# Two plain query outputs ahead of ten factored pairs, and one page group in eight issued by ScalarE

## The chip, the cores and the metric

The kernel runs on one core of a Trainium2 chip. The core has a matrix engine (TensorE, PE in the profile) with its own weight loads (PEld), a vector engine (VectorE, DVE), an activation engine (ScalarE, ACT), a general engine (GpSimd, POOL) and a sync engine (SyncE, SP) that here only issues DMAs. DMAs are issued from SP, ACT or POOL. Each engine takes its instructions strictly in the order in which the program lists them for it. TensorE writes to PSUM, of which there are eight banks; everything else lives in SBUF or in DRAM.

The metric is the device time of one execution in microseconds. Before the change it is 1930.89, the median of three runs from 1927.16 to 1934.16.

## The reference, cut to what matters

One layer of a decoder, for 1024 prompt rows and 32 sample rows (8 sequences of 4), so R = 1056 rows of width 1024:

```python
h = rmsnorm(x, g_norm1) * (1 + scale1) + shift1
za, zq, zkv, zg, zm = jnp.split(h @ w_in, SPLIT_IDX, axis=-1)
u, v = jnp.split(jax.nn.gelu(za), 2, axis=-1)            # gated by W_s: ya
q = zq.reshape(B, T, B_HEADS, HEAD_DIM)
yb = nsa_attention(q, kv_rows, win_rows, ...)            # compressed, selected, window
gate_a, gate_b = jnp.split(jax.nn.sigmoid(zm), 2, axis=-1)
mixed = (gate_a * (ya @ w_branch_a) + gate_b * (yb @ w_branch_b)) @ w_out
x = x + gate1 * mixed
h2 = rmsnorm(x, g_norm2) * (1 + scale2) + shift2         # then ConvFFN, final norm
```

For the sample rows the attention looks at a paged cache: 64 pages of 128 rows for each of 8 sequences. Every 64 rows of two of its four slots go through a small network (`compress_blocks`: a sum over the 64 rows with w1, a gelu, then w2), which gives one compressed key and value per block. The kernel must read all 512 pages for that, 128 KB each.

## The kernel before, in words

All large products are done in float32 precision out of two rounded parts: x = hi + lo, w = hi + lo, and three matmuls hi·hi, hi·lo, lo·hi. `split` and `weight_parts` make the parts: a cast on ScalarE (L332), a subtraction on VectorE (L333). h is kept as eight tiles of hi and eight of lo (`hh`, `hl`), 128 rows of the contraction each and 1056 columns.

An output tile is 128 output features by 1056 columns. `dense` computes one plainly: three column chunks of 384, 384 and 288 (`CH`), eight tiles of h, three matmuls each. The four u tiles are made so (L701 to L724), and each is then multiplied by the spatial gate on GpSimd (L721) and stored (L722).

After them come 22 output tiles in pairs: 4 of queries, 16 of merge gates, 2 of keys. `pair` (L874) computes two output tiles together by a factored form. It cuts the contraction into two halves and the first 608 columns into two blocks of `HQ` = 304, so that h has four blocks B11, B12, B21, B22, and it forms seven block products in place of eight: with B11, B21, B22, with a sum block that takes B12's place, and with three more sum blocks T2, T3, T4. The last 448 columns are done plainly (`rest`). Each block product is 12 matmuls of 304 columns, so a pair has 84 of these and 48 of 448 columns. The sums over weights (s1 to s4) are made on GpSimd.

The sums over h do not exist when the pairs begin. `sums_of(k)` (L825) makes T2, T3 and T4 for one of four tiles; `last_sums` (L841) then overwrites B12 in place, after which a plain product over these columns is no longer possible. Each sum is cut into parts again by `parts_into` (L822 on ScalarE, L823 on VectorE). The first pair therefore has an order of its own (`opening`): all plain products first, with the sums built meanwhile, then the products that need sums. The last pair, the keys, also has its own order (`closing`).

Page loading is the other strand. There are 16 compression steps (L554), each over 32 pages, with one page buffer `st` for all of them. `step(n)` (L662) does compression n on TensorE (128 matmuls), its gelu on ScalarE (L569), and then calls `compress_load(n + 1)`. `load_pages` (L516) reads page numbers four at a time into registers (L528) and issues four DMAs (L538); `share` says which groups of four, by their running number modulo eight, ScalarE issues in place of SP: groups 1, 4 and 6 for steps 0 to 3, none for later ones. Groups on ScalarE are ordered behind the gelu of the step before. Each gelu result `g` is used at the start of the next compression (`compress_end`).

SBUF is divided into pools. `S` has 24 slots of 1056 columns; while the pairs run, 16 hold h, 4 hold w1 and 2 the compressed keys and values, so two are free. `W` holds weights: raw tiles, hi and lo. Before the pairs the old `W` is released and a new one with 4 raw, 3 hi and 3 lo tiles takes its place. `TR` holds T2 to T4, two tiles for weight sums, and one further tile `o` of 1056 columns: `out_tile` gives the two outputs of a pair out of the free slots and this tile in turn, so three places in all. An output's place comes free when its store from POOL's queue has landed.

TensorE's order in this part is set by a planner: it goes through the program with a cost model and puts at each point the first instruction of the text that the model holds to be ready. In the attention part the order is written out by hand (`manual_schedule`), where `later(steps, wait)` delays a piece by a count of columns; `US` is 2265 columns.

After the pairs come key tiles (eight copies on ScalarE, L1014 and L1015), the last compression (15), loads of queries and values on SP (L1038, L1051, L1054), and the first attention tile with its scores and exponentials (L1310).

Of the kernel before, what the change touches and what calls it, by code (L numbers as in the profile page):

```python
# [15 lines left out]
R = 1056  # L16
# [3 lines left out]
HQ = 304  # L20
# [33 lines left out]
def step_kernel(tc, A):  # L54
# [51 lines left out]
    def slot(dt=F32):  # L106
        return S([128, R], dt, "S", NS)
# [408 lines left out]
    def load_pages(items, after=None, share=(1, 4, 6), depth=2):  # L516
# [3 lines left out]
        for n in range(0, len(items), 4):  # L520
# [19 lines left out]
            starts.append(d)  # L540

    hidden = []

    paged = {}

    def compress_load(n):
        b, half = n // 2, n % 2
        home = "a"
        st = PG([128, 32, 256], F32, "st", 1)
        load_pages([(st[:, i], A["pcmp"], b * 64 + half * 32 + i) for i in range(32)], freed.get(home),  # L550
                   (1, 4, 6) if n < 4 else ())
        paged[n] = st, home
# [14 lines left out]
    def compress_act(n, ps, home):  # L567
        g = small(128, "pa", 3).rearrange("p (h c) -> p h c", h=2) if n == 15 else PG([128, 2, 64], F32, "g", 1)
        freed[home] = act.activation(g.rearrange("p h n -> p n h"), ps[:, 0:128].rearrange("p (n h) -> p n h", h=2),  # L569
                                     AF.Gelu_apprx_tanh, bias=b1t)  # L570
        hidden.append((n, g))
# [154 lines left out]
    RV.release()  # L726
    W.release()
    W = new_pool("weights2", "right")
    TR = new_pool("tr", "right")
# [9 lines left out]
    YCW = C2([128, 2, 128])  # L739

    def small(w, tag, bufs):
        return C2([128, w], F32, tag, bufs)

# [67 lines left out]
    f32 = lambda x: (x[0].bitcast(F32), x[1].bitcast(F32))  # L811
    homes = [0]

    def out_tile():
        homes[0] += 1
        return TR([128, R], F32, "o", 1) if homes[0] % 3 == 0 else slot()

    def sum_tile(i):
        return TR([128, 512], F32, f"sum{i}", 1)

# [3 lines left out]

    def sums_of(k, e):  # L825

        (h11, l11), (h12, l12), (h21, l21), (h22, l22) = (f32(x[k]) for x in (B11, B12, B21, B22))
        t = TR([128, R], F32, "o", 1)
        f0, f1, d = (t[:, HQ * i:HQ * i + HQ] for i in range(3))
        pool.tensor_tensor(d, l22, l12, op=OP.subtract)  # L830
        dve.tensor_tensor(f0, h22, h12, op=OP.subtract)
        dve.tensor_tensor(f0, f0, d, op=OP.add)
        dve.tensor_tensor(f1, f0, h11, op=OP.add)
        dve.tensor_tensor(f1, f1, l11, op=OP.add)
        parts_into(f1, *T2[k])
        pool.tensor_tensor(e, h21, f1, op=OP.subtract)
        pool.tensor_tensor(e, e, l21, op=OP.add)
        parts_into(f0, *T3[k])
        parts_into(e, *T4[k])

    def last_sums():  # L841

        t = TR([128, R], F32, "o", 1)
        for k in range(4):
            (h11, l11), (h12, l12) = (f32(x[k]) for x in (B11, B12))
            g, d = (t[:, c:c + HQ] for c in ((0, HQ), (HQ, 2 * HQ))[k % 2][0:1] + (2 * HQ,))
            pool.tensor_tensor(d, l12, l11, op=OP.subtract)
            dve.tensor_tensor(g, h12, h11, op=OP.subtract)
            dve.tensor_tensor(g, g, d, op=OP.add)
            parts_into(g, *B12[k])  # L850

    def weight_parts(x):
        hi, lo = (W([128, 512], F32R, tag, 3) for tag in ("hi", "lo"))
        split(x, hi, lo)
        return [[t[:, c:c + 128] for c in range(0, 512, 128)] for t in (hi, lo)]
# [10 lines left out]

    def pair_load(m, n):
        raws = []
        for j, c in ((m, 0), (n, 0), (n, 512), (m, 512)):
            raws.append(W([128, 512], F32, "raw", 4))  # L870
            pool.dma_start(raws[-1], A["w_t"][j][:, c:c + 512])  # L871
        return raws

    def pair(raws, ev, opening=False, closing=False):  # L874

        a11, a21, a22, a12 = raws
        g, t = out_tile(), out_tile()
        first, second, third = slice(0, HQ), slice(HQ, 2 * HQ), slice(2 * HQ, R)
# [16 lines left out]
        yield t, g  # L895
        if opening or closing:
            quarter_products(weight_parts(a21), rest[0:4], plain[1], True, False)
        if opening:
            quarter_products(weight_parts(a22), rest[4:8], plain[1], False, True)
            ev(g[:, third], plain[1])  # L900
            yield
        if not (opening or closing):
# [7 lines left out]
        if closing:  # L910
# [19 lines left out]
            return  # L930
        if opening:
            quarter_products(weight_parts(s2), T2, S, True, True)
            add(t[:, second], S, g[:, first])
        quarter_products(weight_parts(s3), T3, S, False, True)
# [6 lines left out]
        ev(g[:, 0:2 * HQ], g[:, 0:2 * HQ])  # L941
        if not opening:
            quarter_products(w, rest[4:8], plain[1], False, True)
            ev(g[:, third], plain[1])
        quarter_products(weight_parts(s4), B22, Z, False, True)
# [33 lines left out]

    n = 5  # L980
    PAIR = [(4, 5), (6, 7)] + [(10 + 2 * i, 11 + 2 * i) for i in range(8)] + [(9, 8)]
    raws = pair_load(*PAIR[0])
    for i in range(11):
        fn, ev, base = ((query, scaled, 4) if i < 2 else (merge_gate, gate, 10) if i < 10 else
                        (key, lambda o, x: act.copy(o, x), 8))
        work = pair(raws, ev, i == 0, i == 10)
        tiles = next(work)
        if i == 0:
            for k in range(4):
                sums_of(k, tiles[k % 2][:, HQ:2 * HQ])  # L990
            next(work)
            last_sums()
        if i < 10:
            step(n)
            n += 1
        next(work)
        if i < 10:
# [4 lines left out]
        if i in (5, 6, 7, 8):  # L1002
            next(first_blocks, None)
# [17 lines left out]
    def queries(i, l, qf=None):  # L1021
# [15 lines left out]
    qf = slot()[:, 0:512]  # L1037
    sync.dma_start(qf.rearrange("p (j c) -> p j c", j=4),  # L1038
                   q_d[:, :, 128 * TILES[0]:128 * TILES[0] + 128].rearrange("j p c -> p j c"))
    q_first = queries(TILES[0], None, qf)  # L1040
# [8 lines left out]
    qt = [slot() for _ in range(4)]  # L1049
    for j in range(4):  # L1050
        sync.dma_start(qt[j], q_d[j])  # L1051
    VV = [slot(), slot()]
    for i in range(2):
        sync.dma_start(VV[i][:, 0:1024].rearrange("p (k c) -> p k c", c=256),  # L1054
                       A["o_rows"][1][512 * i:512 * i + 512].rearrange("(k p) c -> p k c", p=128))

# [460 lines left out]
    with tc.manual_schedule(engines={mybir.EngineType.PE}):  # L1517
# [6 lines left out]

        later(ending(), US)
        for n in range(len(units) + AHEAD):
# [571 lines left out]
```

## Time and profile before

| | us |
|---|---|
| median of three runs | 1930.89 |
| lowest, highest | 1927.16, 1934.16 |
| profiled execution | 1926.18 |
| its span on the core | 1924.6 |
| TensorE busy in the span | 1828.4 |
| VectorE, ScalarE, GpSimd busy | 1243.1, 840.1, 636.5 |
| granted TensorE clock, mean | 0.988 |

The span runs from the first to the last instruction of the profiled execution; times inside it are counted from its start. A group row gives the source line, engine, operation and operand shapes, the count, then the busy time and the mean duration of one in ns, then the idle time of the engine just before these instructions with what ended it. Matmuls overlap in the pipeline, so the mean of one is longer than the distance between two. A timeline row gives start, length, the first instruction of a run of them, the count, and in brackets the idle time before. In the chain, SPq is the queue of the sync engine: it issues DMAs and is not counted as busy. A stage row gives busy times, the granted clock, the mean busy share of the 16 DMA engines, and GB/s.

### The profile page before, as it was taken

What the parts mean: (1) busy time and instruction counts of PE and PEld (TensorE: products, weight loads), DVE (VectorE), ACT (ScalarE), POOL (GpSimd) and SP (SyncE); (2) the same over time, 40 slices, a digit from 0 to 9 for tenths busy, and PEclk for the clock granted to TensorE, in tenths of its full rate; (3) what the DMA queues carried; (4) which work ended last, traced back from release to release, by engine and by line L of the source; (5) the groups of instructions that cost most, each with busy time, mean ns of one, the idle gap of its engine ahead of it and who ended that gap; (6) DMA issues with size and microseconds to landing.
All of it is one profiled execution on the core that took longest, in us unless ns stands there. A gap on an engine that the chain in (4) does not pass through costs nothing.

```text
span 1924.6 us, 43777 instructions
## 1 busy us (share of the span) xinstructions
PE 1828.4 (95%) x15905; PEld 1701.1 (88%) x15905; DVE 1243.1 (65%) x2547; ACT 840.1 (44%) x1707; POOL 636.5 (33%) x849
## 2 busy tenths in 40 slices
PE   5999989999998999999999999899999999999997
PEld 3999978998997776767789999899999999999997
DVE  7525265233335776776665778999988888757464
ACT  4313122233224654656652366544444444555343
POOL 2410253222232123222211411578766665301010
PEclk8999999999998999999999999999999999999998
DMA  9545455565659678867754455133322222767463
GB/s 335 191 141 173 155 174 185 178 221 187 219 195 300 223 230 288 276 224 237 251 185 179 146 165 170 56 123 123 95 88 76 87 76 93 264 209 231 127 197 104
DMA packets 239031, 345.35 MB, mean 179 GB/s; under 512 B 35264, under 2 KB 173408, under 8 KB 236640
## 3 DMA queue, kind: packets, MB, share of 16 engines
q1 hardware_dynamic: 205936, 260.48, 42.7%
q0 software_dynamic: 21328, 69.70, 10.6%
q10 hardware_dynamic: 11552, 12.37, 2.1%
q8 instruction: 126, 2.06, 0.4%
q14 instruction: 89, 0.73, 0.1%
HBM read 305.17 MB, written 41.43 MB: 180 GB/s over the span
## 4 chain that ended last, share of the span: by engine, by line
PE 73%; DVE 8%; DMA 6%; SPq 4%; issue 4%; ACT 3%; POOL 1%; DVEq 0%; ACTq 0%; POOLq 0%
PE t L63 70%; SPq L538 4%; PE t L67 3%; DVE t L333 2%; DMA t<-pcmp 1%; DMA t<-w_ada 1%; DMA t<-t 1%; DMA t<-psel 1%; ACT t L332 1%; DVE t L1730 1%; DVE t L1853 1%; SPq L528 1%; ACT t L1310 0%; DMA t<-w_t 0%; ACT t L1339 0%
## 5 line engine op out<-in xcount | busy, mean ns | idle before, releaser
L63 PE MATMUL t<-t,t 128*128 128x264 f32 (+12 forms) x15130 | 1754.2, 305 | 78.5 <-DVE t L184 16.2
L63 PEld LDWEIGHTS t<-t,t 128*128 128x128 f32 (+2 forms) x14970 | 1619.8, 168 | 153.8 <-issue 59.5
L333 DVE TENSOR_TENSOR t<-t,t 128x512 fp32r<-128x512 f32 (+5 forms) x523 | 433.6, 836 | 203.9 <-ACT t L332 197.3
L332 ACT CAST t<-t 128x512 fp32r<-128x512 f32 (+5 forms) x589 | 339.1, 593 | 497.5 <-PE t L63 351.4
L67 PEld LDWEIGHTS t<-t,t 128*128 128x128 f32 x746 | 81.0, 143 | 32.3 <-issue 9.0
L1778 DVE TENSOR_TENSOR t<-t,t 128x264 f32<-128x264 f32 (+2 forms) x296 | 92.1, 345 | 26.7 <-PE t L63 23.9
L67 PE MATMUL t<-t,t 128*128 128x128 f32 x746 | 106.5, 278 | 3.0 <-ACT t L1377 1.5
L538 POOL DMA_DIRECT2D t<-psel x128 | 70.6, 552 | 71.7 <-DMA t<-psel 29.2
L881 DVE TENSOR_TENSOR t<-t,t 128x304 f32<-128x304 f32 x55 | 25.9, 473 | 102.1 <-PE t L63 98.7
L1932 POOL TENSOR_TENSOR t<-t,t 128x384 f32<-128x384 f32 (+1 forms) x12 | 14.0, 1198 | 223.2 <-ACT t L1999 223.2
L1339 ACT COPY t<-t 128x512 f32<-128x512 f32 (+1 forms) x112 | 59.6, 569 | 35.3 <-PE t L67 35.2
L1309 DVE TENSOR_REDUCE t<-t 128x1 f32<-128x640 f32 (+3 forms) x64 | 58.8, 920 | 24.4 <-PE t L63 24.0
L1731 DVE SCALAR_TENSOR_TENSOR t<-t,t,t 128x1072 f32<-128x1072 f32 x44 | 74.5, 1692 | 0.0
L1730 DVE SCALAR_TENSOR_TENSOR t<-t,t,t 128x1072 f32<-128x1072 f32 x44 | 69.6, 1582 | 1.9 <-ACT t L1729 1.8
L1729 ACT ACTIVATE t<-t,t 128x1072 f32<-128x1072 f32 x44 | 56.8, 1290 | 31.5 <-DVE t L1778 22.9
L1310 ACT ACTIVATE t<-t,t 128x640 f32<-128x640 f32 (+3 forms) x64 | 56.3, 880 | 23.2 <-DVE t L1309 20.8
L1835 POOL TENSOR_TENSOR t<-t,t 128x1024 f32<-128x1024 f32 x22 | 54.6, 2481 | 20.5 <-ACT t L1834 20.5
L1366 POOL COPY t<-t 128x256 f32<-128x256 f32 x32 | 12.9, 404 | 133.8 <-DVE t L1364 61.4
L871 POOL DMA_DIRECT2D t<-w_t x44 | 24.6, 559 | 93.9 <-DVE t L333 76.9
L569 ACT ACTIVATE t<-t,t 128x128 f32<-128x128 f32 x16 | 7.9, 493 | 99.4 <-PE t L63 99.4
L721 POOL TENSOR_TENSOR t<-t,t 128x512 f32<-128x512 f32 (+1 forms) x12 | 12.1, 1025 | 115.6 <-ACT t L332 86.9
L1609 POOL TENSOR_TENSOR t<-t,t 128x384 f32<-128x384 f32 (+1 forms) x24 | 27.9, 1167 | 64.6 <-DVE t L1608 61.4
(294 smaller groups left out, 1421.0 us busy)
## 6 DMA issues: line engine op xcount, KB each, us to landing
t<-pcmp SPq DMA_DIRECT2D x464, 128.0 KB
t<-psel SPq DMA_DIRECT2D x384, 128.0 KB
t<-w_down SPq DMA_DIRECT2D x120, 256.0 KB
t<-t POOLq DMA_DIRECT2D x54, 528.0 KB, 3.8
t<-w_up SPq DMA_DIRECT2D x96, 256.0 KB
t<-psel POOLq DMA_DIRECT2D x128, 128.0 KB, 3.9
t<-w_ada SPq DMA_DIRECT2D x16, 1024.0 KB
t<-w_out SPq DMA_DIRECT2D x48, 256.0 KB
```

What stands on the lines that cost most here:

```text
L63: return pe.matmul(out, lhsT, rhs, start=start, stop=stop, skip_group_check=skip)
L67: return pe.transpose(out, x, ident)
L332: act.copy(hi, t)
L333: dve.tensor_tensor(lo, t, hi.bitcast(F32), op=OP.subtract)
L538: d = queue.dma_start(dst, src[bass.ds(r, 1)].rearrange("g p c -> p (g c)"))
L1309: dve.tensor_reduce(m4[:, branch, h:h + 1], ps[:, :, 0:w], axis=AX.XY, op=OP.max, negate=True)
L1310: act.activation(P[:, 0:L].rearrange("p (a c) -> p a c", a=2), ps[:, :, 0:w], AF.Exp, bias=m4[:, branch, h:h + 1], accum_out=s4[:, branch, ...
L1339: (act.copy if w > 2 else dve.tensor_copy)(probs[branch, h][:, 128 * k:128 * (k + w)], pt[:, c:c + 128 * w])
L1729: act.activation(acc[:, 0:w], up[:, 0:w], AF.Identity, scale=cw[:, n, 0:1], bias=cw[:, n, 3:4])
L1730: dve.scalar_tensor_tensor(acc[:, 0:w], up[:, 1:1 + w], cw[:, n, 1:2], acc[:, 0:w], op0=OP.mult, op1=OP.add)
L1731: dve.scalar_tensor_tensor(acc[:, 0:w], up[:, 2:2 + w], cw[:, n, 2:3], acc[:, 0:w], op0=OP.mult, op1=OP.add)
L1778: dve.tensor_tensor(o, by4(banks[c][:, c0:c0 + n], n), other(c, c0, n), op=OP.add)
```

## The change

The sums over h are no longer built inside a pair. Query outputs 4 and 5 are computed plainly (`plain_output`), half of the contraction at a time, and `sums_of` is called after each half; `last_sums` follows the second output. Compression 5 stands between the two. Ten pairs follow, the first of them queries 6 and 7; `pair` loses its opening order. In pair 0 compression 6 stands after the second group of products, and in pairs 1 to 8 compressions 7 to 14 stand after the first group.

The weight pool is not released: the pairs use the pool of the dense outputs, with 4 raw, 4 hi and 4 lo tiles of 524 columns. The tile `o` is gone: outputs of a pair and the scratch of the sums all come from the free slots. The differences that T4 is cut from go into the two weight-sum tiles.

From load 4 on, group 1 of each eight is issued by ScalarE. Every gelu result takes the tag `pa` of the small tiles, as only the last one did. The loads of queries and values are ordered behind the gelu of compression 14, and the small step that ends compression 15 is due 6 x US columns into attention and not 1 x US.

```diff
         load_pages([(st[:, i], A["pcmp"], b * 64 + half * 32 + i) for i in range(32)], freed.get(home),
-                   (1, 4, 6) if n < 4 else ())
+                   (1, 4, 6) if n < 4 else (1,))
...
-        g = small(128, "pa", 3).rearrange("p (h c) -> p h c", h=2) if n == 15 else PG([128, 2, 64], F32, "g", 1)
+        g = small(128, "pa", 3).rearrange("p (h c) -> p h c", h=2) 
...
-    W.release()
-    W = new_pool("weights2", "right")
     TR = new_pool("tr", "right")
...
-    def out_tile():
-        homes[0] += 1
-        return TR([128, R], F32, "o", 1) if homes[0] % 3 == 0 else slot()
...
-        t = TR([128, R], F32, "o", 1)
+        t = slot()
         f0, f1, d = (t[:, HQ * i:HQ * i + HQ] for i in range(3))
+        e = sum_tile(k % 2)[:, 0:HQ]
...
-        hi, lo = (W([128, 512], F32R, tag, 3) for tag in ("hi", "lo"))
+        hi, lo = (W([128, WP], F32R, tag, 4)[:, 0:512] for tag in ("hi", "lo"))
...
+    def plain_output(raws, ev, between):
+        out = slot()
+        banks = [pA()[:, 0:b - a] for a, b in CH]
+        for half in range(2):
+            w = weight_parts(raws[half])
+            for (a, b), ps in zip(CH, banks):
+                x = [(hh[k][:, a:b], hl[k][:, a:b]) for k in range(4 * half, 4 * half + 4)]
+                quarter_products(w, x, ps, half == 0, half == 1)
+                if half:
+                    ev(out[:, a:b], ps)
+            between(half)
+        return out
...
-        g, t = out_tile(), out_tile()
+        g, t = slot(), slot()
...
-    PAIR = [(4, 5), (6, 7)] + [(10 + 2 * i, 11 + 2 * i) for i in range(8)] + [(9, 8)]
+    plain_raws = raw_weights(((4, 0), (4, 512), (5, 0), (5, 512)))
+    query(0, plain_output(plain_raws[0:2], scaled, lambda half: sums_of(half)))
+    step(5)
+    query(1, plain_output(plain_raws[2:4], scaled, lambda half: sums_of(2 + half)))
+    last_sums()
+    PAIR = [(6, 7)] + [(10 + 2 * i, 11 + 2 * i) for i in range(8)] + [(9, 8)]
     raws = pair_load(*PAIR[0])
-    for i in range(11):
+    for i in range(10):
...
+        work = pair(raws, ev, i == 9)
+        next(work)
+        if 0 < i < 9:
+            step(6 + i)
+        next(work)
         if i == 0:
+            step(6)
...
+    fourteen = freed["a"]
+    with behind([fourteen]):
+        sync.dma_start(qf.rearrange("p (j c) -> p j c", j=4),
...
-        later(ending(), US)
+        later(ending(), US * 6)
```

More of the change, by code (lines that the diff above doesn't have):

```diff
@@ L540, in load_pages, with small @@
             starts.append(d)
+    def small(w, tag, bufs):
+        return C2([128, w], F32, tag, bufs)
     hidden = []
@@ L739, in step_kernel @@
     YCW = C2([128, 2, 128])
-    def small(w, tag, bufs):
-        return C2([128, w], F32, tag, bufs)
     def blocks(gr, bank):
@@ L811, in step_kernel @@
     f32 = lambda x: (x[0].bitcast(F32), x[1].bitcast(F32))
-    homes = [0]
-    def out_tile():
-        homes[0] += 1
-        return TR([128, R], F32, "o", 1) if homes[0] % 3 == 0 else slot()
-    def sum_tile(i):
-        return TR([128, 512], F32, f"sum{i}", 1)
+    sum_tile = lambda i: TR([128, 512], F32, f"sum{i}", 1)
     def parts_into(x, hi, lo):
@@ L823, in parts_into, with sums_of @@
         dve.tensor_tensor(lo, x, hi.bitcast(F32), op=OP.subtract)
-    def sums_of(k, e):
+    def sums_of(k):
         (h11, l11), (h12, l12), (h21, l21), (h22, l22) = (f32(x[k]) for x in (B11, B12, B21, B22))
-        t = TR([128, R], F32, "o", 1)
+        t = slot()
         f0, f1, d = (t[:, HQ * i:HQ * i + HQ] for i in range(3))
+        e = sum_tile(k % 2)[:, 0:HQ]
         pool.tensor_tensor(d, l22, l12, op=OP.subtract)
@@ L841, in last_sums @@
     def last_sums():
-        t = TR([128, R], F32, "o", 1)
+        t = slot()
         for k in range(4):
@@ L865, in step_kernel, with raw_weights, pair_load, pair @@
     rest = [tuple(t[:, 2 * HQ:R] for t in (hh[k], hl[k])) for k in range(8)]
-    def pair_load(m, n):
+    def raw_weights(items):
         raws = []
-        for j, c in ((m, 0), (n, 0), (n, 512), (m, 512)):
-            raws.append(W([128, 512], F32, "raw", 4))
+        for j, c in items:
+            raws.append(W([128, WP], F32, "raw", RAWS)[:, 0:512])
             pool.dma_start(raws[-1], A["w_t"][j][:, c:c + 512])
         return raws
-    def pair(raws, ev, opening=False, closing=False):
+    def pair_load(m, n):
+        return raw_weights(((m, 0), (n, 0), (n, 512), (m, 512)))
+    def plain_output(raws, ev, between):
[10 more added lines that the diff above has]
+        return out
+    def pair(raws, ev, closing=False):
         a11, a21, a22, a12 = raws
-        g, t = out_tile(), out_tile()
+        g, t = slot(), slot()
         first, second, third = slice(0, HQ), slice(HQ, 2 * HQ), slice(2 * HQ, R)
@@ L895, in pair @@
         yield t, g
-        if opening or closing:
+        if closing:
             quarter_products(weight_parts(a21), rest[0:4], plain[1], True, False)
[L898 to L902, printed above, removed]
+        else:
             quarter_products(weight_parts(s2), T2, S, True, True)
@@ L930, in pair @@
             return
-        if opening:
-            quarter_products(weight_parts(s2), T2, S, True, True)
-            add(t[:, second], S, g[:, first])
         quarter_products(weight_parts(s3), T3, S, False, True)
@@ L941, in pair @@
         ev(g[:, 0:2 * HQ], g[:, 0:2 * HQ])
-        if not opening:
-            quarter_products(w, rest[4:8], plain[1], False, True)
-            ev(g[:, third], plain[1])
+        quarter_products(w, rest[4:8], plain[1], False, True)
+        ev(g[:, third], plain[1])
         quarter_products(weight_parts(s4), B22, Z, False, True)
@@ L978, in key @@
                 pool.dma_start(A["o_wsk"][b][:, 508:512], kr[:, NP + 4 * b:NP + 4 * b + 4])
-    n = 5
-    PAIR = [(4, 5), (6, 7)] + [(10 + 2 * i, 11 + 2 * i) for i in range(8)] + [(9, 8)]
+    plain_raws = raw_weights(((4, 0), (4, 512), (5, 0), (5, 512)))
[4 more added lines that the diff above has]
+    PAIR = [(6, 7)] + [(10 + 2 * i, 11 + 2 * i) for i in range(8)] + [(9, 8)]
     raws = pair_load(*PAIR[0])
-    for i in range(11):
-        fn, ev, base = ((query, scaled, 4) if i < 2 else (merge_gate, gate, 10) if i < 10 else
+    for i in range(10):
+        fn, ev, base = ((query, scaled, 4) if i < 1 else (merge_gate, gate, 10) if i < 9 else
                         (key, lambda o, x: act.copy(o, x), 8))
-        work = pair(raws, ev, i == 0, i == 10)
-        tiles = next(work)
-        if i == 0:
[L989 to L997, printed above, removed]
+        work = pair(raws, ev, i == 9)
[3 more added lines that the diff above has]
+        next(work)
+        if i == 0:
+            step(6)
+        if i < 9:
             raws = pair_load(*PAIR[i + 1])
@@ L1001, in step_kernel @@
             fn(j - base, x)
-        if i in (5, 6, 7, 8):
+        if i in (4, 5, 6, 7):
             next(first_blocks, None)
@@ L1037, in step_kernel @@
     qf = slot()[:, 0:512]
-    sync.dma_start(qf.rearrange("p (j c) -> p j c", j=4),
-                   q_d[:, :, 128 * TILES[0]:128 * TILES[0] + 128].rearrange("j p c -> p j c"))
+    fourteen = freed["a"]
+    with behind([fourteen]):
+        sync.dma_start(qf.rearrange("p (j c) -> p j c", j=4),
+                       q_d[:, :, 128 * TILES[0]:128 * TILES[0] + 128].rearrange("j p c -> p j c"))
     q_first = queries(TILES[0], None, qf)
@@ L1049, in step_kernel @@
     qt = [slot() for _ in range(4)]
-    for j in range(4):
-        sync.dma_start(qt[j], q_d[j])
     VV = [slot(), slot()]
-    for i in range(2):
-        sync.dma_start(VV[i][:, 0:1024].rearrange("p (k c) -> p k c", c=256),
-                       A["o_rows"][1][512 * i:512 * i + 512].rearrange("(k p) c -> p k c", p=128))
+    with behind([fourteen]):
+        for j in range(4):
+            sync.dma_start(qt[j], q_d[j])
+        for i in range(2):
+            sync.dma_start(VV[i][:, 0:1024].rearrange("p (k c) -> p k c", c=256),
+                           A["o_rows"][1][512 * i:512 * i + 512].rearrange("(k p) c -> p k c", p=128))
     psum.release()
```

## The prediction

> **What bounds the kernel now.** The page first: which engine is busy, and the chain that ended last.
>
> ```profile
> span 1924.6 us, 43777 instructions
> PE 1828.4 (95%) x15905; PEld 1701.1 (88%) x15905; DVE 1243.1 (65%) x2547; ACT 840.1 (44%) x1707; POOL 636.5 (33%) x849
> ...
> PE 73%; DVE 8%; DMA 6%; SPq 4%; issue 4%; ACT 3%; POOL 1%; DVEq 0%; ACTq 0%; POOLq 0%
> PE t L63 70%; SPq L538 4%; PE t L67 3%; DVE t L333 2%; DMA t<-pcmp 1%; DMA t<-w_ada 1%; DMA t<-t 1%; DMA t<-psel 1%; ACT t L332 1%; DVE t L1730 1%; DVE t L1853 1%; SPq L528 1%; ACT t L1310 0%; DMA t<-w_t 0%; ACT t L1339 0%
> ```
>
> TensorE sets the time, but 4% of the chain is SP issuing page loads (L538). The edits lie between the last dense output and the first attention tile, so next the busy times by stage: the opening pair, the ten later pairs, the last compression, and the way into attention.
>
> ```profile
> core 0: us, PE busy (x) PEld busy (x) DVE busy (x) ACT busy (x) POOL busy (x), PEclk, DMA share, GB/s
> 252.30:303.80 51.50, 39.19 (x287) 34.03 (x288) 41.62 (x63) 15.69 (x33) 29.33 (x31) 0.87 0.54 169
> 303.80:594.30 290.50, 283.34 (x2573) 270.39 (x2573) 104.04 (x187) 83.13 (x151) 85.90 (x102) 1.00 0.63 200
> 594.30:602.70 8.40, 6.25 (x60) 5.93 (x62) 4.09 (x13) 2.79 (x9) 0.54 (x1) 0.80 0.89 281
> 602.70:616.60 13.90, 8.22 (x117) 7.57 (x117) 10.89 (x17) 11.22 (x13) 5.23 (x10) 0.91 1.04 395
> ```
>
> The opening keeps TensorE busy for 39 of 51.5 us, at a granted clock of 0.87; the later pairs lose 7.2 of 290.5 at full clock. Which wait ends last there, from the groups of the opening and from TensorE's timeline:
>
> ```profile
> L63 PE MATMUL t<-t,t 128*128 128x304 f32 x86 | 17.2, 341 | 7.9 <-ACT t L822 5.6 <-DVE t L881 1.8 <-DVE t L823 0.4
> L63 PE MATMUL t<-t,t 128*128 128x448 f32 x62 | 15.9, 403 | 4.5 <-DVE t L333 4.3 <-ACT t L332 0.2
> ```
> ```profile
> 260.34 17.01 PE L63 MATMUL t<-t,t 128*128 128x448 f32 x186 [1.82 <-DVE t L333]
> ...
> 283.64 1.64 PE L63 MATMUL t<-t,t 128*128 128x304 f32 x3 [3.60 <-ACT t L822]
> ...
> 297.18 9.02 PE L63 MATMUL t<-t,t 128*128 128x448 f32 x56 [1.75 <-DVE t L333]
> ```
> ```profile
> 343.70 95.78 PE L63 MATMUL t<-t,t 128*64 128x128 f32 x853 [1.65 <-issue]
> 440.71 31.23 PE L63 MATMUL t<-t,t 128*64 128x128 f32 x284 [1.23 <-DMA t<-pcmp]
> 473.38 12.72 PE L63 MATMUL t<-t,t 128*64 128x128 f32 x167 [1.43 <-DMA t<-pcmp]
> ...
> 504.45 30.16 PE L63 MATMUL t<-t,t 128*64 128x128 f32 x308 [0.95 <-DMA t<-pcmp]
> 536.36 57.93 PE L63 MATMUL t<-t,t 128*64 128x128 f32 x532 [1.75 <-DMA t<-pcmp]
> 596.45 13.87 PE L63 MATMUL t<-t,t 128*64 128x128 f32 x166 [2.16 <-DMA t<-pcmp]
> ...
> 616.56 8.76 PE L63 MATMUL t<-t,t 128*128 128x320 f32 x43 [3.24 <-ACT t L1310]
> ```
>
> So the opening waits for the h sums (L822, L823) and for its first weights (L333); from 440 on every compression finds its pages late. Compressions start 32.67, 31.07 and 31.91 us apart: mean 31.9.
>
> **The change part by part.** First the price of a column, from a stretch without waits, 351.3 to 375.8:
>
> ```profile
> L63 PE MATMUL t<-t,t 128*128 128x304 f32 x100 | 14.8, 302 | 0.0
> L63 PE MATMUL t<-t,t 128*128 128x448 f32 x51 | 11.4, 369 | 0.0
> ```
>
> And of two compressions, between 192 and 260:
>
> ```profile
> L63 PE MATMUL t<-t,t 128*64 128x128 f32 x256 | 14.9, 274 | 0.0
> ```
>
> The first is 100 x 304 + 51 x 448 = 53,248 columns in 24.5 us, 0.460 ns each. A pair is 84 x 304 + 48 x 448 = 47,040 columns, 21.6 us. A compression is 7.5 us.
>
> *Opening pair becomes two plain outputs.* In its stage 86 x 304 + 62 x 448 = 53,920 columns are 24.8 us; with the compression 32.3 of 51.5 us. The loss is 19.2 us: 12.4 idle, the rest slow clock after the idle. Two plain outputs are 2 x 24 x 1056 = 50,688 columns, 23.3 us, 1.7 more than the pair. Plain products need no sums, and since the weight pool stays, their raw tiles need not wait for the old pool's readers. Gain 19.2 - 1.7 = 17.5.
>
> What hides the sums: TensorE has 252.3 + 23.3 + 7.5 (compression 5) + 8.3 (the next pair's first 18,048 columns) = 291.4 before it needs T2. Their scratch is now one of two free slots; the other holds query 0, so they wait for the last u tile's store:
>
> ```profile
> L722 POOL DMA_DIRECT2D t<-t x4: 585/602/627, 199.9 to 255.8; - x4
> ...
> DMA to landing us min/median/max: 3.0/4.1/4.6
> L834 DVE TENSOR_TENSOR t<-t,t x4: 461/468/474, 264.8 to 282.6; 128x304 f32<-128x304 f32 x4
> ```
>
> The store lands by 260.4. One set of sums follows another every (282.6 - 264.8) / 3 = 5.9 us; four end at 284, 7 us early. The last sums overwrite B12, which query 1's first half still reads until about 277; the new B12 is due another 13 us after T2. From both sides this costs 0 to 10 us; I take 2, since the margin is positive but both scratch and outputs share two slots.
>
> *One page group in eight goes to ScalarE.* SP's timeline for one load now, and for an early load that already has three groups on ScalarE:
>
> ```profile
> 383.56 20.51 SPq L538 DMA_DIRECT2D t<-pcmp  x32
> ```
> ```profile
> 181.44 15.45 SPq L538 DMA_DIRECT2D t<-pcmp  x20
> ```
>
> A group costs SP at most 20.51 / 8 = 2.56 us; taking three away saved 5.06, 1.69 each. I take the middle, 2.1: the cycle of compression, issue and landing falls from 31.9 to 29.8. TensorE's own work per cycle is 21.6 + 7.5 = 29.1. So the waits on pages, 5.4 us, and the one marked issue before compression 7 (1.65, the cycle before them) go, and 0.7 us a cycle may be left, 7 cycles, 4.9 at most, nothing if the order of TensorE absorbs it; I take 4. The two prices of a group give 0.2 and 1.1 us a cycle. ScalarE pays four issues a load, behind the activation that ends a compression, and the casts of the next weights queue behind them. Four weight buffers cover that, and ScalarE is busy 83 of 290.5 us; without that cover it is the same 2.1 us a cycle. The number of DMAs stays.
>
> The Trainium skill (DMA: Bandwidth & Descriptors, "Issuing engines are not separate DMA queues") speaks against much: a second issuing engine saves only sequencer time, since all transfers share 16 engines. By that rule the saving is the full issue time if issuing sets the pace, and none if the transfers do; the second is a rival below.
>
> *The last compression.* Its wait of 2.16 goes: the last pages are issued about a cycle after compression 14, and 30 us of pair work lie between. The stage from 594.3 to 602.7 also holds the closing pair's last product (12 x 304 columns, 1.7 us); the other 4.5 of its 8.4 us are compression run ahead of that product, which should now come first. What follows hangs on that product, through ScalarE:
>
> ```profile
> 603.66 1.05 ACT L1014 CAST t<-t 64x1024 fp32r<-64x1024 f32 x1 [2.47 <-DVE t L881]
> ...
> 612.21 0.49 ACT L569 ACTIVATE t<-t,t 128x128 f32<-128x128 f32 x1
> ```
>
> Eight copies of key tiles hold ScalarE until 612.2 and TensorE resumes at 616.56, 13.9 us after the product ended at 602.7. That distance I keep. So the later ending step (6 x US instead of US) gains nothing: it moves an idle time that the exponentials end anyway. The query loads held behind compression 14 cost nothing: SP issues them after the last page already.
>
> *Outputs in two slots instead of three tiles.* The next pair's first copy must wait until an output of the last pair has been stored. TensorE needs that copy done 6.6 us into the pair (24 x 448 + 12 x 304 = 14,400 columns).
>
> ```profile
> L881 DVE TENSOR_TENSOR t<-t,t 128x304 f32<-128x304 f32 x55 | 25.9, 473 | 102.1 <-PE t L63 98.7 <-ACT t L985 2.2 <-DMA t<-w_t 1.1
> L967 DVE TENSOR_SCALAR t<-t 128x1056 f32<-128x1056 f32 x16 | 12.1, 759 | 0.1
> L951 ACT ACTIVATE t<-t 128x304 f32<-128x304 f32 x16 | 7.0, 440 | 1.9 <-DVE t L881 1.8
> ```
> ```profile
> L968 POOL DMA_DIRECT2D t<-t x16: 538/562/578, 363.6 to 571.5; - x16
> ...
> DMA to landing us min/median/max: 2.9/3.9/6.2
> ```
>
> Add 0.47, activation 0.44, scaling 0.76, landing 3.9 (from the issue): 5.6 us, and the copy about 0.4: 6.0, just in time. At the longest landing, 6.2, it is 1.7 late. 0 to 1.7 a pair, nine pairs: 0 to 15; I take 2, by the median. Moving the compression's g into a shared tag of three costs nothing: the blocks hold two at most while it holds one; without a free one the activation waits.
>
> *Sum.* At the closing pair's last product: -17.5 - 5.4 - 1.65 - 2.16 - 4.5 = -31.2; new waits 2 + 4 + 2 = 8; net -23. The profiled execution took 1926.2 (span 1924.6 and 1.6 around it), 4.7 below the median of 1930.9. So 1903 on its scale, 1908 on the median's.
>
> **The rivals.**
>
> *Transfers set the page pace.* For: during a load the DMA engines are busy 0.83.
>
> ```profile
> 416.00:440.00 24.00, 23.49 (x144) 22.36 (x143) 9.69 (x15) 8.27 (x16) 7.72 (x10) 1.00 0.83 265
> ```
>
> Against: not full, and three groups on ScalarE did shorten a load. Then the cycle stays 31.9 and TensorE waits 2.8 in each of 7 cycles: 19.6 in place of 4, gain 7, 1923. This is what the skill's rule gives if transfers are the limit; the trace agrees only in part. Chance 0.11.
>
> *The sums are not hidden.* If their scratch comes free only when query 0 has been stored (ends at 264, lands about 270), they end near 294 and the last sums follow; the first pair then waits, with the slow clock, some 10 us instead of 2: 1916. For: two slots for three users. Against: the u store frees one by 260.4. Chance 0.13.
>
> *The two output slots stop TensorE: slower.* Near the end of the stage, where the DMA share is 0.9 and more, landing takes longer:
>
> ```profile
> L975 POOL DMA_DIRECT2D o_k<-t x2: 539/539/539, 596.4 to 604.1; - x2
> ...
> DMA to landing us min/median/max: 6.1/7.5/8.9
> ```
>
> If faster page issue fills the DMA engines so that gate outputs land at 8.9, each of nine pairs stalls 0.47 + 0.44 + 0.76 + 8.9 + 0.4 - 6.6 = 4.4 us, about 40 in place of 2: the gain of 23 becomes a loss of 15, 1946. It decides against the change from a landing of about 7.3 us on (2.8 a pair). Against: none of the 16 gate stores took over 6.2. Chance 0.08.
>
> **How the numbers follow.** Forecast 0.65: 1908. Its own range is 1900 (no new wait) to 1918 (18 us of them: 5 pages, 5 sums, 8 outputs). The three rivals hold 0.32; 0.03 is for anything that cancels out. A change below 0.3% (5.8 us) can't be told from none here. Faster takes the forecast, the sums, and most of the page rival: 0.85. Same 0.07: the rest of the page rival and the cancelling case. Slower 0.08. The range, 1897 to 1925, reaches 3 us past each end of what it holds, since the runs before differ by that much from their median; it leaves out the slow rival and a tail of the others.
>
> **What would show it.** In the changed profile: no wait on L822 between the last dense output and the first pair, and a clock near 1.00 there; compressions about 29.5 us apart; the wait on pages before them under 1 us; SP's issue of 28 pages in 18 to 19 us; the closing pair's last product near 580 and the first attention waits 23 us earlier than 616.6; the same distances after it. Wrong would be: a cycle of 32 us; waits of TensorE on the copy at the start of each pair; a T2 product that waits; or an attention stage that gives the gain back.

## The result, and the profile after

The changed kernel takes 1901.24 us, the median of four runs (1894.15 to 1902.34), beside 1929.03 (1926.31 to 1934.16) for the kernel before in the same set. The ratio is 0.9845, with a 95% interval from 0.9812 to 0.9878: 27.8 us gained, where 23 were forecast. The profiled execution took 1901.98 us. Of six executions with the key tiles late, an experiment below, one took 2968.6 us at a granted clock of 0.558; the median there holds it, the ratio does not. Many line numbers from L542 on are shifted: L822 and L823 are now L813 and L814, L881 is L889, L569 is L572, L1310 is L1313; L538, L332 and L333 are as before.

First the page of the changed kernel, busy times and the chain:

```profile
span 1900.0 us, 43806 instructions
PE 1823.7 (96%) x15917; PEld 1701.5 (90%) x15917; DVE 1227.0 (65%) x2537; ACT 834.7 (44%) x1702; POOL 634.2 (33%) x845
...
PE 77%; DVE 11%; ACT 4%; issue 3%; DMA 3%; POOL 1%; SPq 1%; DVEq 0%; ACTq 0%; POOLq 0%
```

SP's issuing fell from 4% to 1% of the chain. Next the busy times by stage, in the columns of the prediction: the two plain outputs with compression 5, the ten pairs, the last compression with the closing product, and the way into attention.

```profile
255.00:286.40 31.40, 31.40 (x284) 30.77 (x284) 16.89 (x32) 7.95 (x18) 16.09 (x18) 1.00 0.60 189
286.40:572.00 285.60, 285.60 (x2590) 272.80 (x2589) 108.89 (x201) 84.42 (x157) 92.74 (x107) 1.00 0.66 210
572.00:577.20 5.20, 4.22 (x55) 3.85 (x56) 2.74 (x8) 2.17 (x7) 0.57 (x2) 1.00 0.95 296
577.20:591.40 14.20, 8.10 (x114) 7.36 (x114) 12.09 (x21) 11.67 (x16) 5.95 (x10) 0.90 1.02 382
```

TensorE's timeline over the whole of it:

```profile
239.80 227.95 PE L63 MATMUL t<-t,t 128*64 128x128 f32 x2075
467.58 0.27 PE L784 MATMUL t<-t,t 128*128 128x128 f32 x1
467.61 104.44 PE L63 MATMUL t<-t,t 128*128 128x448 f32 x940
573.03 11.49 PE L63 MATMUL t<-t,t 128*64 128x128 f32 x162 [0.98 <-DMA t<-pcmp]
584.89 0.78 PE L63 MATMUL t<-t,t 128*128 128x320 f32 x4 [0.37 <-DVE t L1017]
591.44 0.90 PE L63 MATMUL t<-t,t 128*128 128x320 f32 x2 [5.77 <-ACT t L1313]
```

There is no idle time from the last dense outputs to compression 15: busy equals span in both of the first stages, at the full clock, and the only wait is 0.98 us on the last pages.

Where the gain lies follows from the stage rows, those of before in the prediction; the work of the next pair's first 3.2 us (6,880 columns) is taken out of the opening of before and put back into its pairs.

| stage | before, us | after, us | difference | forecast |
|---|---|---|---|---|
| opening and compression 5 | 51.5 - 3.2 = 48.3 | 31.4 | -16.9 | -17.5 + 2 |
| ten pairs | 290.5 + 3.2 = 293.7 | 285.6 | -8.1 | -7.05 + 6 |
| compression 15, closing product | 8.4 | 5.2 | -3.2 | -6.66 |
| on to the first attention waits | 13.9 | 14.2 | +0.3 | 0 |
| sum | | | -27.9 | -23.2 |

From TensorE's resume to the end of the span it is 1308.0 before (616.56 to 1924.6) and 1308.6 after (591.44 to 1900.0). The profiled times differ by 24.2, not 27.9, because this execution reached the first plain output 2.7 us later (255.0 against 252.3). That part varies among executions of either kernel: compression 0 starts at 101.9 in before and 104.9 in after, and when the changed kernel ran again at 103.1. The experiments are therefore read over one stretch, from the start of compression 4 to the resume.

### The profile page after: what moved, and what is told of

It is laid out like the page before. It is cut to its first block, busy times and chain, and to the rows that moved or that the text cites. A ratio compares the mean times of both kernels' runs of the same rounds, so it can differ in the third digit from the quotient of the medians.

```text
span 1900.0 us, 43806 instructions
## 1 busy us (share of the span) xinstructions
PE 1823.7 (96%) x15917; PEld 1701.5 (90%) x15917; DVE 1227.0 (65%) x2537; ACT 834.7 (44%) x1702; POOL 634.2 (33%) x845
## 3 DMA queue, kind: packets, MB, share of 16 engines
q0 software_dynamic: 21328, 69.70, 10.7%
## 4 chain that ended last, share of the span: by engine, by line
PE 77%; DVE 11%; ACT 4%; issue 3%; DMA 3%; POOL 1%; SPq 1%; DVEq 0%; ACTq 0%; POOLq 0%
PE t L63 74%; PE t L67 3%; DVE t L333 3%; DMA t<-psel 1%; DVE t L1733 1%; DMA t<-t 1%; DVE t L1781 1%; DVE t L1734 1%; SPq L538 1%; DVE t L1856 1%; ACT t L332 0%; ACT t L1313 0%; DMA t<-w_up 0%; ACT t L1342 0%; DVE t L414 0%
## 5 line engine op out<-in xcount | busy, mean ns | idle before, releaser
L63 PE MATMUL t<-t,t 128*128 128x264 f32 (+14 forms) x15142 | 1749.1, 304 | 58.1 <-DVE t L184 16.2
L333 DVE TENSOR_TENSOR t<-t,t 128x512 fp32r<-128x512 f32 (+5 forms) x518 | 423.8, 826 | 214.2 <-ACT t L332 203.1
L332 ACT CAST t<-t 128x512 fp32r<-128x512 f32 (+6 forms) x584 | 335.3, 592 | 466.4 <-PE t L63 309.3
L538 POOL DMA_DIRECT2D t<-psel x128 | 71.2, 556 | 71.8 <-PE t L63 25.4
L889 DVE TENSOR_TENSOR t<-t,t 128x304 f32<-128x304 f32 x50 | 23.4, 472 | 67.9 <-PE t L63 57.5
L1313 ACT ACTIVATE t<-t,t 128x640 f32<-128x640 f32 (+3 forms) x64 | 56.2, 879 | 24.1 <-DVE t L1312 20.0
L1759 POOL TENSOR_TENSOR t<-t,t 128x512 f32<-128x512 f32 x21 | 27.9, 1329 | 64.4 <-DMA t<-w_up 31.8
L572 ACT ACTIVATE t<-t,t 128x128 f32<-128x128 f32 x16 | 7.9, 494 | 88.8 <-PE t L63 88.8
```

The costliest lines, as they stand in the source:

```text
L63: return pe.matmul(out, lhsT, rhs, start=start, stop=stop, skip_group_check=skip)
L332: act.copy(hi, t)
L333: dve.tensor_tensor(lo, t, hi.bitcast(F32), op=OP.subtract)
L538: d = queue.dma_start(dst, src[bass.ds(r, 1)].rearrange("g p c -> p (g c)"))
L1313: act.activation(P[:, 0:L].rearrange("p (a c) -> p a c", a=2), ps[:, :, 0:w], AF.Exp, bias=m4[:, branch, h:h + 1], accum_out=s4[:, branch, ...
```

## The experiments

The table has all runs; the stretch and TensorE's busy time in it come from the stage view of each run's profile, resume to end from the same timelines. Two runs resumed in another way, so columns are left empty. With the queue's order written out, a kernel's lines are up to 8 higher (L575 is the gelu L572 there). Resume to end differs by up to 4 us among runs with the same order there; that was not followed.

| run | median, us | ratio (95%) | compression 4 to resume | busy in it | resume to end |
|---|---|---|---|---|---|
| kernel before | 1927.1 to 1929.0 | | 384.2 | 356.9 | 1308.0 |
| group only | 1928.84 | 1.0006 (0.9987 to 1.0024) | 377.3 | 357.2 | 1318.2 |
| group only, queue ordered | 1919.87 | 0.9961 (0.9945 to 0.9977) | 378.1 | 358.0 | 1307.6 |
| opening only, queue ordered | 1914.17 | 0.9933 (0.9917 to 0.9949) | 368.2 | 350.5 | 1310.9 |
| changed, pool renewed | 1909.23 | 0.9891 (0.9868 to 0.9915) | 364.6 | 352.1 | 1311.2 |
| changed, no group | 1915.58 | 0.9934 (0.9906 to 0.9961) | 359.7 | 348.6 | 1318.3 |
| changed, no group, queue ordered | 1910.46 | 0.9909 (0.9888 to 0.9931) | 362.6 | 350.2 | 1307.6 |
| changed | 1901.24 | 0.9845 (0.9812 to 0.9878) | 355.7 | 348.6 | 1308.6 |
| changed, again | 1899.10 | 0.9847 (0.9820 to 0.9874) | 354.3 | 348.4 | 1309.4 |
| changed, three groups | 1955.30 | 1.0139 (1.0116 to 1.0161) | 414.5 | 376.5 | 1308.5 |
| changed, 15 behind the product | 1897.84 | 0.9839 (0.9813 to 0.9865) | 354.5 | 348.2 | 1308.5 |
| the same again | 1899.80 | 0.9853 (0.9834 to 0.9871) | 355.5 | 348.3 | 1311.6 |
| changed, key tiles late | 1902.53 | 0.9866 (0.9837 to 0.9894) | | | |
| changed, ending early | 1898.80 | 0.9851 (0.9833 to 0.9868) | 355.1 | 349.0 | |

### The page group alone

The kernel before, with the group alone:

```diff
-                   (1, 4, 6) if n < 4 else ())
+                   (1, 4, 6) if n < 4 else (1,))
```

> The kernel before with one edit: from load 4 on, group 1 of each eight is issued by ScalarE. Two-chain theory (TensorE's work of 29.1 us a cycle, and the page cycle of 31.9 us before, about 29.8 with the edit): the waits on pages of 1.23, 1.43, 0.95, 1.75 and 2.16 us and the 1.65 us before compression 7 shrink to about 1 us in all, the opening keeps its loss of 19 us; 8 us faster than before, about 1921. Rival, transfers set the page pace: compressions stay 32 us apart and the time stays within 2 us of before. Rival, the opening is the whole gain: also no change.

It gained nothing: 1928.84. But inside the stretch it did gain 6.9 us (384.2 to 377.3); from the resume to the end it then took 10.2 longer. SP's timeline of this run behind the last pages shows why:

```profile
598.84 0.35 SPq L1226 DMA_DIRECT2D t<-w_ada  x1
599.24 3.97 SPq L1051 DMA_DIRECT2D t<-t  x4
603.26 1.24 SPq L1054 DMA_DIRECT2D t<-o_rows  x2
604.54 4.75 SPq L1226 DMA_DIRECT2D t<-w_ada  x1
...
620.12 21.10 SPq L538 DMA_DIRECT2D t<-psel  x30
```

In this program the planner put one load of w_ada ahead of the q and v loads (L1051, L1054). That load goes into the page buffer, so it waits until compression 15 has read it; q and v, which wait for nothing, stood behind it and were issued at 599 and not during compression 15. The selected pages (psel) come later too, and in attention TensorE then waits for w_ada (us in total, number of waits, longest):

```profile
PE t L63 <- DMA t<-w_ada: 4.3, 2, 3.0
```

That is 4.3 of the 10 us; where the others arise was not followed wait by wait. The test of the reading is the same kernel with the old order on this queue: w_ada, and in the same way wk, wv and psel, stand behind the last load of v.

```diff
-        sync.dma_start(VV[i][:, 0:1024].rearrange("p (k c) -> p k c", c=256),
+        kept.append(sync.dma_start(VV[i][:, 0:1024].rearrange("p (k c) -> p k c", c=256),
...
-            sync.dma_start(st[:, p0:p0 + 2048], A["w_ada"][ch][:, p0:p0 + 2048])
+            with behind(kept[-1:]):
+                sync.dma_start(st[:, p0:p0 + 2048], A["w_ada"][ch][:, p0:p0 + 2048])
```

> The kernel before with ScalarE issuing one page group of eight, as in the run with the group alone (1928.8 us, ratio 1.0006), and with an order on SyncE's queue: the loads of the selected and new pages that wait for a page buffer (w_ada, wk, wv, psel) stand behind the loads of q and v, as they do in the kernel before. Nothing is left out. Theory (the group gains some 9 us inside the stage, TensorE resuming at 607.9 us in place of 616.6, and gave 10 us back because a w_ada load that waits for compression 15 held the q and v loads behind it): the 10 us of the way from the resume to the end go away, so about 1919 us, ratio 0.995. Rival (the queue's order is harmless and the 10 us belong to something else that the group changes, for example ScalarE's time): about 1929 us, ratio 1.000.

```profile
588.04 1.76 SPq L1054 DMA_DIRECT2D t<-t  x4
589.90 2.67 SPq L1057 DMA_DIRECT2D t<-o_rows  x2
600.65 0.81 SPq L1232 DMA_DIRECT2D t<-w_ada  x2
...
613.11 23.79 SPq L541 DMA_DIRECT2D t<-psel  x36
```

q and v go out at 588, psel seven us earlier, and resume to end is 1307.6 again. The median falls by 9 us to 1919.87, as the theory had it. So the group alone is worth some 8 us, and the order of the queue decides whether they arrive.

### The change without the page group

The changed kernel, with the group given back:

```diff
-                   (1, 4, 6) if n < 4 else (1,))
+                   (1, 4, 6) if n < 4 else ())
```

> The changed kernel with all pages from load 4 on issued by SP again. Two-chain theory: the page cycle is 31.9 us again, so from compression 5 at 267 the fifteenth starts at about 267 + 10 x 31.9 = 586 and not at 573; about 13 us slower than the changed kernel, 1914, and TensorE waits on pages before most compressions. Rival, the opening is the whole gain (TensorE's order absorbs late pages): within 3 us of the changed kernel, 1901 to 1904.

1915.58, as forecast, but for a second reason as well: here too a w_ada load came ahead of q and v, and resume to end is 1318.3. With the queue ordered as above:

> The changed kernel with all page groups of compressions 4 to 15 issued by SyncE, as in the run without the group (1915.6 us, ratio 0.9934), and with the same order on SyncE's queue: w_ada, wk, wv and psel behind the loads of q and v. Nothing is left out. Theory (of the 14 us that the group was worth in the changed kernel only 4.8 lie in the stage, and 10 come from the order of the queue): about 1906 us, ratio 0.988, some 5 us over the changed kernel. Rival (the group itself is worth all 14): 1915 us, ratio 0.993.

Resume to end is 1307.6, a second time 10.7 less. The profiled execution gained only 6.6 of that, because the stretch came out 2.9 longer and the part before it 1.2, and the median fell by 5, to 1910.46, between the theory and the rival. What the group is worth in the changed kernel is 7 to 8 us by the stretch of this run (362.6 against 355.7 and 354.3), 4 to 5 by that of the run without the order (359.7), and 9 to 11 by the medians. The page waits in this run, beside 1.0 in the changed kernel:

```profile
PE t L63 <- DMA t<-pcmp: 7.9, 6, 2.3
```

### The weight tiles' pool, and the opening by itself

The changed kernel with the pool made anew, and the queue ordered as above:

```diff
+    W.release()
+    W = new_pool("weights2", "right")
...
-        hi, lo = (W([128, WP], F32R, tag, 4)[:, 0:512] for tag in ("hi", "lo"))
+        hi, lo = (W([128, 512], F32R, tag, 3) for tag in ("hi", "lo"))
...
```

> The changed kernel with the pool of the weight tiles given back and made anew ahead of the outputs, with 3 pairs of split tiles and 4 raw ones of 512 columns, as the kernel before has it; the order of SyncE's queue (q and v first) is held as in the changed kernel. Nothing is left out. Theory (the 4.3 us before the first plain product, the waits on the split weights, come from the new pool waiting for the old one's readers): those waits come back, 2.5 to 4.5 us, so about 1904 to 1906 us, ratio 0.987. Rival (the time went with the pairs' own sums, and the pool is no cause): 1901 us, the same as the changed kernel.

Keeping the pool is worth more than either guess: 1909.23, 8 to 10 us slower than the changed kernel. GpSimd's waits show the plain outputs' first weights held up until TensorE is through with the old pool, and ScalarE's show the first split behind them:

```profile
POOL t L868 <- PE t L63: 10.1, 1, 10.1
```
```profile
ACT t L332 <- DMA t<-w_t: 4.2, 2, 3.8
```

Yet on TensorE that costs only 0.44 us. Most of the rest is pages again, over the whole stage, and one of these waits (2.28 us) was followed by five us at a granted clock of 0.66:

```profile
PE t L63 <- DMA t<-pcmp: 5.2, 4, 2.3
```

Whether that comes from three split pairs in place of four, or from the later start, these runs don't tell apart. With the group taken away as well, the plain outputs are what is left:

> The changed kernel with the page group given back to SyncE and the weight tiles' pool given back and made anew, so that the two plain outputs with the sums beside them are what is left of the change (beside the g tile and the order of the last loads); w_ada, wk, wv and psel stand behind the loads of q and v, as in both kernels. Nothing is left out. Theory A (the three parts add up: the pool is worth 9 us, 1909.2 against 1899.1 to 1901.2, the group 9, 1910.5 against the same, and the opening the rest, 28 less 18): about 1918 us, ratio 0.995. Theory B (the opening is worth the 17.5 us of the prediction, and pool and group only share what is left): about 1911 us, ratio 0.991. Theory C (without pool and group the page load of compression 5 and the weight splits hold TensorE at the opening as the missing sums did): within 3 us of the kernel before, 1925 to 1928 us.

1914.17 lies between A and B. The parts don't add up: the opening alone gains 13 us (16 in the stretch); then the pool adds 3.7 without the group (1914.2 to 1910.5) and 10.1 with it (1909.2 to 1899.1), and the group adds 4.9 without the kept pool and 11.4 with it (1910.5 to 1899.1). The 3.7 is not clear of the noise, for the intervals of its two runs overlap. TensorE's waits on pages, which the quicker stage wants sooner, say the same: 8.8 us in this run with neither, 7.9 with the pool alone, 5.2 with the group alone, and 1.0 only with both.

> The changed kernel once more, to stand beside the others of this set. Nothing is left out. 1901 us, ratio 0.985 by every theory.

1899.10, which shows how far two sets agree.

### Three groups on ScalarE

The changed kernel with three groups for every load, and the queue ordered:

```diff
-                   (1, 4, 6) if n < 4 else (1,))
+                   (1, 4, 6))
```

> The changed kernel with ScalarE issuing three page groups of eight (1, 4 and 6) for compressions 4 to 15 as for the first four; the order of SyncE's queue is held (q and v first). Nothing is left out. Theory (TensorE waits on pages for 1.0 us in the whole stage and is the bound; a still quicker issue has nothing to hide): 1901 us, ratio 0.985, the same as the changed kernel within 3 us. Rival 1 (the quicker issue shortens the closing waits as well): 1897 us. Rival 2 (twelve DMAs of each load on ScalarE block it, up to 3 us at a time for four of them, and with it the copies that free the accumulation banks, so TensorE waits): 1905 us or more.

1955.30: rival 2, and far beyond its number. ScalarE's timeline, its waits, and TensorE's waits in that order:

```profile
337.77 0.49 ACT L575 ACTIVATE t<-t,t 128x128 f32<-128x128 f32 x1 [6.24 <-PE t L63]
338.57 9.57 ACTq L541 DMA_DIRECT2D t<-pcmp  x12
348.25 1.66 ACT L332 CAST t<-t 128x512 fp32r<-128x512 f32 x3 [9.99 <-DMA t<-pcmp]
```
```profile
ACT t L332 <- DMA t<-pcmp: 80.0, 8, 10.3
```
```profile
PE t L63 <- ACT t L332: 30.0, 9, 4.2
```

Twelve DMAs take ScalarE 9.57 us, in which it runs no cast, and the casts of the next weights wait behind them. In the changed kernel four DMAs take 1.8 to 3.0 us a load, and the same place reads:

```profile
307.21 1.84 ACTq L538 DMA_DIRECT2D t<-pcmp  x4
309.15 1.31 ACT L332 CAST t<-t 128x512 fp32r<-128x512 f32 x2 [2.25 <-DMA t<-pcmp]
```

Twelve DMAs on ScalarE are not harmful everywhere. In the same run load 4 stands beside dense outputs; it holds ScalarE longer, and TensorE is busy without a break from 208 to 230 (the same holds for load 5, 10.79 us at 239.63):

```profile
211.13 10.21 ACTq L541 DMA_DIRECT2D t<-pcmp  x12
```
```profile
208.00:230.00 22.00, 22.00 (x177) 21.54 (x173) 5.04 (x7) 4.74 (x10) 5.48 (x7) 1.00 0.74 226
```

A likely reason is how long one split of 512 weight columns lasts. In a dense output it serves 4 x 3 x 1056 columns, 5.8 us at the prediction's price of a column; a pair of 21.6 us uses up eight splits, 2.7 us each. With three of four buffers ahead, that is an estimate of 17.5 us of cover there and 8.1 in the pairs, and the twelve DMAs lie between. No run changed the number of buffers, so this is argued and not shown.

The stretch is 58.8 us longer than in the changed kernel. Only 30.9 of that are idle (414.5 - 376.5 against 355.7 - 348.6); 27.9 are busy time for nearly the same products. The granted clock over the stretch is 0.94 against 1.00, and 0.06 x 414.5 gives an estimate of some 25 us, most of it. One wait and the five us behind it:

```profile
348.92 32.44 PE L63 MATMUL t<-t,t 128*128 128x304 f32 x268 [4.23 <-ACT t L332]
```
```profile
348.90:353.90 5.00, 4.98 (x18) 4.85 (x19) 2.17 (x4) 1.01 (x2) 1.10 (x2) 0.50 0.82 260
```

The granted clock is 0.50 behind the wait. A wait on pages in the run with the opening only, and the five us behind it:

```profile
331.07 63.19 PE L63 MATMUL t<-t,t 128*64 128x128 f32 x564 [1.60 <-DMA t<-pcmp]
```
```profile
331.10:336.10 5.00, 5.00 (x95) 5.00 (x97) 0.47 (x2) 0.00 (x0) 2.55 (x2) 1.00 0.21 66
```

There the clock stays at 1.00, though not behind every wait of this length, as the last section shows.

### The last compression and the way into attention

Compression 15 behind the closing pair's last product (`ended` holds that product's last matmul):

```diff
-    compress_act(*compress(15))
+    with behind(ended):
+        fifteen = compress(15)
+    compress_act(*fifteen)
```

> The changed kernel with compression 15 ordered on TensorE behind the closing pair's last product. There, 0.98 us of wait and about 2.2 us of compression 15 still stand ahead of that product. If the way into attention hangs on that product through ScalarE's eight key copies, the product ends 3.2 us earlier and TensorE resumes 3.2 us earlier: 1898. Rival, it hangs on the end of compression 15 and its gelu: no gain, 1901.

> The kernel of the run with compression 15 ordered behind the closing pair's last product, once more: 1897.8 us there, beside 1901.2 and 1899.1 us for the changed kernel. Nothing is left out. Theory (the 2.2 us by which that product ran behind compression 15 are gained, less a new wait of 1.6 us): 1898 us, 1 to 3 us below the changed kernel. Rival (what the order gains, the new wait takes): 1900 us, the same.

1897.84 and 1899.80, against 1901.24 and 1899.10: no difference that these intervals can tell. The timeline of the first of the two suggests why:

```profile
572.68 11.88 PE L63 MATMUL t<-t,t 128*128 128x304 f32 x166 [1.59 <-DVE t L892]
589.25 1.03 PE L63 MATMUL t<-t,t 128*128 128x320 f32 x3 [4.69 <-ACT t L1318]
```

The product comes first, but must wait 1.59 us for VectorE; in the changed kernel the 0.98 us on the pages and 2.2 us of compression 15 stand in that place. The stretch is 354.5 and 355.5 against 355.7 and 354.3.

Then the second half of the key tiles behind the first scores, so that the exponentials need not wait for eight copies:

```diff
     R3 = new_pool("r3", "right")
-    key_tiles(1)
...
+            if n == 0 and r == 0:
+                key_tiles(1)
```

> The changed kernel with the four key copies of the window branch on ScalarE moved behind the first scores of attention. TensorE now waits 5.77 us for the first exponentials, which stand behind eight copies of 1.05 us and one activation. If the copies are what it waits for, the first exponential comes 4.2 us earlier; as the window scores then wait for the moved copies, 2 to 4 us of it remain: 1898. Rival: the copies are needed soon anyway and only move the wait: 1901.

1902.53, the rival. The first exponential does come 4.2 us earlier, 13.3 us after compression 15 starts and not 17.5 (582.47 - 569.20 here, 590.50 - 573.03 in the changed kernel). But TensorE, which has its first scores at 581, then waits for the copies themselves:

```profile
581.12 0.78 PE L63 MATMUL t<-t,t 128*128 128x320 f32 x4 [0.44 <-DVE t L1017]
586.38 0.64 PE L63 MATMUL t<-t,t 128*128 128x320 f32 x1 [4.48 <-ACT t L1015]
```

Last the later ending:

```diff
-        later(ending(), US * 6)
+        later(ending(), US)
```

> The changed kernel with the last compression's end due as early as in the kernel before (one unit in place of six). Nothing is left out. Theory (the move of the ending costs and gains nothing): 1901 us, ratio 0.985. Rival (the later ending keeps its two products and two VectorE additions out of the first attention steps, which are short of both): 1904 us or more.

1898.80: the move costs and gains nothing that these runs can tell.

## Why the prediction was right, and where it was not

**Right in sign, cause and size.** 1901.24 lies inside the range and inside the forecast's own range (1900 to 1918), near its low end, 7 under the forecast of 1908. That the miss is no larger is partly luck: two terms were wrong in opposite directions, by 7 and 2.5 us.

**The opening, -17.5.** Measured -16.9, with no wait on the sums and a clock of 1.00. But "since the weight pool stays, their raw tiles need not wait" was right about the mechanism and too narrow: taking the pool away costs 8 to 10 us, with 5.2 us of waits on pages later on, which the prediction had booked under the page group.

**The new waits, +8.** This is the term that was mis-sized: 1.0 was measured. That alone would have made the gain 30; the closing term gave 2.5 less than forecast (4.2 without the page wait, in place of 6.66), and with the small differences of the other stages it is 27.9 where 23 were expected. The sums cost 0 in place of 2: L813 and L814 release no wait of TensorE. The pages cost 1.0 in place of 4. The two output slots cost 0 in place of 2, although copies do wait for stores in the changed kernel. The stores' own row, and two of the three groups of waits on them, ScalarE's and VectorE's:

```profile
DMA to landing us min/median/max: 2.9/4.2/5.8
```
```profile
ACT t L897 <- DMA t<-t: 7.4, 3, 4.2
```
```profile
DVE t L889 <- DMA t<-t: 7.2, 2, 3.6
```

Waits of up to 4.2 us stayed off TensorE. The slack that the prediction put at 0.6 us must have been larger; the planner's order is where it may come from, which was not tried.

**The page group.** The mechanism held, but a group is worth less on SP than its two prices, 1.7 and 2.6 us. SP's part of a load takes 17.05 to 20.85 us, where 18 to 19 were expected; over loads 4 to 15 the mean is 19.1, beside 20.6 for 32 pages in the kernel before, so a group saves 1.5. The longest load and the shortest:

```profile
401.36 20.85 SPq L538 DMA_DIRECT2D t<-pcmp  x28
...
433.92 17.05 SPq L538 DMA_DIRECT2D t<-pcmp  x28
```

The rival in which transfers set the pace (1923) is out: the DMA share rose from 0.63 to 0.66 as the waits went. The Trainium skill (DMA: Bandwidth & Descriptors, "Issuing engines are not separate DMA queues") says that a second issuing engine saves only sequencer time. That holds here, and that time was what bound: 8 us with the group alone. The other side is the second engine's own time, which cost 54 us with three groups.

"Compressions about 29.5 us apart" was a badly chosen sign. They are 29.3 to 32.6 apart, 31.0 in the mean (267.13 to 545.86, nine gaps), with TensorE busy throughout. Once nothing waits, the distance shows only where the planner put them among the pairs. This may also be why the 4 us of page waits didn't come: the prediction set a page cycle of 29.8 against 29.1 us of work, but a cycle of 31.9 - 1.5 = 30.4 (an estimate) met a mean distance of 31.0.

**Compression 15, -4.5.** "That product should now come first" failed. The product still ran from 575.25 to 577.18, behind 2.2 us of compression 15, so the stage gained 3.2 and not 6.66. Ordering it first gains nothing that the runs can tell either, so the term was wrong as a gain and not only as a forecast of the order.

**What was put at nothing.** The 13.9 us to the resume came out as 14.2, and the later ending as nothing. Written without the order behind compression 14, the changed program has the same instructions in the same order on every engine; that edit does nothing here. What the prediction didn't ask is which load heads SP's queue then. Before and after it is the same; in two of the runs it was not, and that cost 10 us.

**The slow rival (1946).** It named the output stores. A loss against the kernel before (28 us) did come in the run with three groups, by another path: an edit next to this one, on the engine that issues.

## What to carry to other kernels

Where an engine that computes also issues DMAs, price the issues as its own work: four cost 1.8 to 3.0 us here and were covered; twelve cost over 9, harmless beside the dense outputs, but in the pairs they stopped TensorE through the casts behind them. After any change of timing, look at what stands at the head of each issuing queue: a load that waits for a buffer holds every load behind it, and here that hid the whole gain of an edit that had worked. Judge an edit over the stretch that it touches as well as by the total, since two edits that feed the same wait (pages) are worth little singly and much together.

## What the runs showed of the hardware

A wait of TensorE can cost more than its length. In the run with three groups, eight of nine waits from 2.7 to 4.2 us were followed by five us at a granted clock of 0.50 to 0.67 and one (2.94 us) by 1.00. Shorter waits went either way. In the run with the opening only, the five us behind waits of 1.6 to 2.3 us had 1.00; but behind the wait of 2.16 us at 596.45 in the kernel before, and behind one of 2.28 us with the pool renewed, the clock was 0.66:

```profile
596.45:601.45 5.00, 5.00 (x51) 4.83 (x52) 2.23 (x8) 2.38 (x8) 0.47 (x1) 0.66 1.00 305
```
```profile
269.60:274.60 5.00, 4.98 (x64) 5.00 (x66) 4.34 (x13) 0.89 (x2) 1.65 (x3) 0.66 0.29 111
```

So no length marks the border in these runs. The Trainium skill (TensorE: Matmul & The Clock Gate, "Why this matters for your kernels") advises against idle gaps of more than about 3 us between bursts of matmuls; the trace agrees, and has waits of 2.2 to 2.7 us that already cost clock. In the run with three groups this made 30.9 idle us part of a loss of 58.8.
